# Experts' loads take places that come free piece by piece in the first stage; the inversion does both directions in one thread

## The chip, the cores and the metric

The kernel runs on one core of a Trainium2 chip. Its time is device time in microseconds, the median of 3 runs: 1031.37 us before the change (1030.21 to 1035.38).

## The reference, cut to what matters

All is float32, with 256 tokens of width 1024. A first block is a bidirectional gated delta rule (GDN) with an output projection and a LayerNorm, then 32 experts in 4 groups with top-1 group and top-2 experts, a LayerNorm and an embedding gate. A second block of two layers follows (an mLSTM layer and a sparse attention layer); the change does not touch what they compute.

```python
def _gated_delta_rule(q, k, v, beta, g):      # per chunk; once forward, once on the reversed sequence
    lhs = eye + jnp.einsum("nbhik,nbhjk->nbhij", kb, k) * decay * (1.0 - eye)
    u = solve(lhs, v * beta[..., None])        # unit lower triangular
    ...
x = _layernorm(ALPHA * x + gdn, ...)
for grp in range(4):                           # the experts
    h = silu(einsum("td,edf->tef", xt, w_gate[grp])) * einsum("td,edf->tef", xt, w_up[grp])
    out = out + einsum("tef,efd->td", h * comb[:, grp, :, None], w_down[grp])
x = _layernorm(ALPHA * x + out, ...)
x = x + sigmoid(x @ pe_w_gate) * (p @ pe_w_proj)
```

## The kernel before, in words

**Who sets the order.** The program is written as threads (Python generators) that a planner, `Sched` (L141), interleaves when the kernel is built. A thread asks for an engine (`yield "pe"`), waits for an event (`Wait`) or asks for buffers (`Alloc`); the planner keeps a modelled clock of each engine, of the DMA and of when each buffer comes free, picks the earliest thread (among nearly equal ones that of the smallest priority number), and writes its instructions out in that order. So a change of a modelled cost or of a buffer class can change the order of other work. On the chip each engine runs its instructions in the order written and waits by semaphores.

**Weights.** All weights come through one list of units of 1024 floats per partition (512 KB), loaded strictly in the list's order by one thread, `_load` (L488), on SP's queue. A unit asks for a place from the classes in its `places`. Dense weights are split by `_split` (L505) into a high and a low part in two places of class `hl`, and the raw place is free again; a unit marked late or full is used as it was loaded where the split doesn't come in time. Experts' weights (`m_gu`, 128 units, and `m_dn`, 64) are used as they are loaded. SP also issues the few other loads, among them x and two LayerNorm rows in `finish` (L1430).

**Places before.** 4 `raw` and 6 `hl` last for the whole program. 15 `moe_raw` and 4 `moe_hl` are opened by `moe_slots` (L470) in `hand_over` (L1367), when the GDN's buffers `la`, `e`, `t2`, `raw2` and `tap` are all done with. 8 more `moe_raw` (named `moe_raw_m` in the trace) and 2 `x_raw` are opened when the experts' stage begins. These are 39. The experts' units of the first two of eight steps may take `moe_raw` alone; the others take all classes, and wait for the last output-projection weights to be split. The residual r and the gathered tokens XG have buffers of their own.

**The first stage (GDN).** `main` (L1380) runs projections in the order of `GDN_ORDER` (L1475): q and k of head pairs 0 to 3, then v and z, then heads 4 to 7, z4 to z7, and the output projection o0 to o7. The heads are treated in two batches of four (`bt` 0 and 1). For each batch `base` (L1167) inverts 32x32 diagonal blocks column by column on VectorE (`columns`, L1210), `lev` (L1228) builds the 64x64 and 128x128 inverses from them by matmuls, and `solve` (L1305) applies them for each head pair; a solve frees the two `la` buffers of its pair, and the second batch's pairs take these. TensorE fills the rest with projections.

**The levels of the inversion.** `lev` is spawned four times, for 2 batches and 2 directions d. A step is a run of small matmuls into PSUM (class `bank`) and then evictions by ScalarE and VectorE, which the next step needs. Step 1: 32 matmuls of 32x32, half of them on one row group of the array, then half on another, all into the bank `px`. Step 2: per block two matmuls that read the same rows and write different columns, into banks `pt` and `pS`. Steps 3 and 4: 16 matmuls of 64x64 each, on one half of the rows. In the trace step 1 is `bank<-t,la`, step 2 `bank<-Tm,t` and `bank<-t,Tm`, step 3 `bank<-Tm,la`, step 4 `bank<-Sm,Tm`. A float32 matmul leaves two records.

**The experts' stage.** `Moe.main` (L2265): `ranks` and `group` make selection matrices, `gather` (L2092) collects up to 32 tokens per expert into XG, `up` (L2177) of step i multiplies them with 16 units of `m_gu` for four experts side by side on four column groups, `down` (L2198) with 8 units of `m_dn`, `scatter` adds to r. In the last `up`, `second_turn` (L2286) has a branch for crowded experts; at its end SP waits for all its loads, and only then the eight loads of `p_gate` for the embedding gate follow, into `raw` places.

Of the kernel before, what the change touches and what calls it, by code (L numbers as in the profile page):

```python
# [1 line left out]

# [43 lines left out]
MOE_RAW = 15  # L46
MORE_RAW = 8
# [93 lines left out]
class Sched:  # L141
# [60 lines left out]
    def mm(self, out, lhsT, rhs, first, last):  # L202
        self.nc.tensor.matmul(out, lhsT, rhs, start=first, stop=last, skip_group_check=True)  # L203
        n, m = size(rhs), size(lhsT)
        one = lhsT.dtype == F32R
        if n == 512 and m == 32:

            self.array(n, n)
            return
        self.array(max(n, 2 * m) if one else 4 * max(n, m) if n > 64 else 2.4 * n if m < 128 else max(4 * n, 2 * m),  # L210
                   (n if one else 4 * n) * rhs.shape[0] / 128.0, 0.0125 if one else 0.0025)
# [48 lines left out]

    def drop(self, *classes):
        for c in classes:
            del self.slots[c], self.pools[c]
# [33 lines left out]
    def _grant(self):  # L297

        again = True
        while again:  # L300
            again = False
            for t in sorted(self.threads, key=lambda t: (t.prio, t.seq)):
# [7 lines left out]
                elif isinstance(w, Alloc):  # L310
                    free = [s for c in (w.cls if isinstance(w.cls, tuple) else (w.cls,))
                            for s in self.slots.get(c, ())]
                    if len(free) >= w.n:
                        got = []
                        for s in sorted(free, key=lambda s: s.time)[:w.n]:
                            self.slots[s.cls].remove(s)
                            if isinstance(s.tag, int):
                                tile = self.pools[s.cls][:, s.tag]
# [59 lines left out]
class Unit:  # L378
# [4 lines left out]
    def __init__(self, name, src, more="", n=1024, whole=False, late=False, full=False,  # L383
                 places=None):
        self.name, self.src, self.more, self.n, self.whole, self.late = name, src, more, n, whole, late
        self.full, self.low, self.places = full, False, places or ("raw", more + "raw")
        self.sent, self.loaded = Event(), Event()
# [7 lines left out]
class Env:  # L395


    def __init__(self, tc, aps, ctx):
# [6 lines left out]
        self.res = ctx.enter_context(tc.tile_pool(name="res", bufs=1))  # L405
        S.slot_class("raw", self.wp, 4)
# [4 lines left out]
    def gate_slots(self):  # L411
# [4 lines left out]
        for x in s["gate_hl"]:  # L416
# [53 lines left out]
    def moe_slots(self):  # L470
# [3 lines left out]
        for cls, n in (("moe_raw", MOE_RAW), ("moe_hl", 4)):  # L474
# [6 lines left out]
    def start_weights(self, units, hold={}):  # L481

        self.units, self.at, self.hold = units, 0, hold
        for i, u in enumerate(units):
            u.index = i
        self.S.spawn(self._load(), 0)

    def _load(self):  # L488
# [15 lines left out]

    def _split(self, u):  # L505
        S = self.S
        hl = yield Alloc(("hl", u.more + "hl"), [1024], F32R, 2)
        yield Wait(u.loaded)
# [274 lines left out]
    def transposed(self, x, tb, h, l):  # L783

        yield Wait(*[self.S.spawn(self.turn(x, tb, h, l, c, Event()), 1) for c in (0, 4)])

    def turn(self, x, tb, h, l, c, done):
# [4 lines left out]
        for i in range(4):  # L792
            S.tr(p[:, i, :], x[:, tb, 128 * (c + i):128 * (c + i) + 128], self.ident)
# [84 lines left out]
class Gdn:  # L878


    def __init__(self, K, ctx):
# [5 lines left out]

        self.early = ExitStack()
        E = self.early.enter_context(K.stage("gdn_early", "right"))
        self.early_classes = ("la", "e", "t2", "raw2", "tap")  # L890
        for cls, n in zip(self.early_classes, (8, 4, 4, 4, 2)):
            K.S.slot_class(cls, E, n)
        K.S.slot_views("zx", K.res.tile([128, 4, 512], F32, name="x1", tag="x1"))
        self.LA, self.lev_ev, self.O = {}, {}, {}
# [10 lines left out]
        self.solved = [Event() for _ in range(8)]  # L905
# [169 lines left out]
    def qk_head(self, m, bank):  # L1075
# [18 lines left out]
        las = yield Alloc("la", [2, 3, 2, 128], n=2)  # L1094
# [6 lines left out]
        for d in range(2):  # L1101
            la = las[d]
# [64 lines left out]
    def base(self, bt):  # L1167
# [14 lines left out]
        tmp = yield Alloc("raw2", [512])  # L1182
# [45 lines left out]
    def lev(self, bt, d):  # L1228

        K, S = self.K, self.S  # L1230
        v, s, Sm, Tm = S.v, S.s, None, None
        yield Wait(self.base_ev[bt])
        Sm, Tm = self.Sm, self.Tm
        s32, t32 = self.AB if d == 0 else self.AB[::-1]
        u = slice(16 * d, 16 * d + 16)

        def lower(i):
            return self.LA[4 * bt + (i % 16) // 4, d][:, (i // 2) % 2, i % 2, 0]

        def span(pr):  # L1240
            return 64 * pr + 32 * d, 64 * pr + 32 * (1 - d)
# [8 lines left out]
        for pr, e in ((0, "act"), (1, "dve")):  # L1250
            f, t = span(pr)
            o = Tm[t:t + 32, u, 32 * d:32 * d + 32]
            yield e
            if pr:
                v.tensor_copy(o, px[t:t + 32])
            else:
                s.activation(o, px[t:t + 32], AF.Copy)
        S.free(px)
        yield Wait(self.diag_ev[bt])
        pt, pS = yield Alloc("bank", [16, 32], n=2)  # L1260
        for pr in range(2):
            f, t = span(pr)
            yield "pe"
            for i in range(16 * d, 16 * d + 16):
                x = Tm[t:t + 32, i, 32 * d:32 * d + 32]
                st = s32[t:t + 32, i, :]
                S.mm(pt[t:t + 32, i % 16, :], st, x, True, True)
                S.mm(pS[f:f + 32, i % 16, :], x, st, True, True)
        for pr in range(2):
            f, t = span(pr)  # L1270
            yield "act"
            s.activation(Tm[t:t + 32, u, 32 * d:32 * d + 32], pt[t:t + 32], AF.Copy, scale=-1.0)
            yield "dve"
            v.tensor_scalar(Sm[f:f + 32, u, t:t + 32], pS[f:f + 32], -1.0, None, op0=OP.mult)
        S.free(pt, pS)
        f, t = 64 * d, 64 * (1 - d)
        px = yield Alloc("bank", [8, 64], n=2)
        for half in range(2):
            yield "pe"
            for i in range(16 * d + 8 * half, 16 * d + 8 * half + 8):  # L1280
                S.mm(px[half][t:t + 64, i % 8, :], lower(i)[f:f + 64, t:t + 64], Tm[f:f + 64, i, :], True, True)
# [1764 lines left out]
```

## Time and profile before

| | |
|---|---|
| median of 3 runs | 1031.37 us |
| the profiled execution | 1031.94 us |
| its span | 1030.2 us |
| mean granted clock of TensorE | 0.972 |
| TensorE busy | 972.1 us (94%) |
| VectorE busy | 619.2 us (60%) |
| ScalarE busy | 484.9 us (47%) |
| bytes moved by DMA | 205.39 MB, mean 199 GB/s |

The span is what the profiler saw from the first to the last instruction; the execution's own time is 1.7 us longer. Times in the trace are microseconds from the span's start. Busy matmuls overlap, so TensorE's share is not its share of peak. A granted clock of 1.00 is 2.4 GHz, of 0.50 it is 1.2 GHz.

### The profile page before, as it was taken

To read this page: it belongs to the slowest core of one execution; us is meant where nothing else is said; L and a number is where in the kernel's file an instruction comes from. 1 tells how busy PE (TensorE), PEld (TensorE's weight loads), DVE (VectorE), ACT (ScalarE), POOL (GpSimd) and SP (SyncE) were. 2 spreads that over 40 slices of the span, in tenths; PEclk is the share of its full clock that TensorE was granted. 3 is DMA by queue.
4 is the path that set the end of the run, shared out by engine and by line. 5 is a ranking of instruction groups with operands and counts; after the bars stand their busy time and mean duration, and the time that the engine had idled before them with its cause. 6 is when DMAs were issued, how large, how long until landed. Compare 5 with 4: busy or idle time off the path is not lost. (4 is left out here: it accounts for less than half of the span.)

```text
span 1030.2 us, 17204 instructions
## 1 busy us (share of the span) xinstructions
PE 972.1 (94%) x6837; PEld 752.1 (73%) x6837; DVE 619.2 (60%) x1148; ACT 484.9 (47%) x897; POOL 114.2 (11%) x124
## 2 busy tenths in 40 slices
PE   8999989999899989999998788999999999998998
PEld 6778889888679765423221158999999988986886
DVE  7978865699944650221111086688677765687673
ACT  3888484794224422111110156576665444545561
POOL 2133130023000110000000050000000000004230
PEclk9999879999899989999999989999999999999999
DMA  6423411233332999999999953644554455732321
GB/s 222 144 82 104 143 43 42 63 123 102 123 104 77 408 416 381 416 414 416 415 415 415 403 191 127 202 150 162 165 163 157 158 176 164 257 114 71 123 83 41
DMA packets 56681, 205.39 MB, mean 199 GB/s; under 512 B 6417, under 2 KB 6801, under 8 KB 56209
## 3 DMA queue, kind: packets, MB, share of 16 engines
q1 hardware_dynamic: 56304, 204.02, 54.7%
q8 instruction: 56, 0.92, 0.4%
q10 hardware_dynamic: 288, 0.19, 0.1%
q14 instruction: 33, 0.26, 0.1%
HBM read 203.14 MB, written 1.05 MB: 198 GB/s over the span
## 5 line engine op out<-in xcount | busy, mean ns | idle before, releaser
L203 PE MATMUL dbank<-xh,hl 128*128 128x256 f32 x1072 | 216.4, 294 | 0.0
L203 PEld LDWEIGHTS dbank<-xh,hl 128*128 128x128 f32 x1072 | 173.7, 193 | 6.8 <-issue 4.9
L126 DVE TENSOR_TENSOR hl<-raw,hl 128x1024 fp32r<-128x1024 f32 x106 | 130.2, 1234 | 41.2 <-ACT hl L126 35.5
L203 PE MATMUL dbank<-xl,hl 128*128 128x256 f32 x536 | 152.7, 285 | 0.0
L126 ACT ACTIVATE hl<-raw 128x1024 fp32r<-128x1024 f32 x99 | 104.3, 1057 | 82.0 <-PE dbank L203 60.0
L203 PE MATMUL dbank<-hl,xh 128*128 128x256 f32 (+1 forms) x504 | 116.9, 317 | 0.9 <-ACT xh L126 0.9
L203 PEld LDWEIGHTS dbank<-xl,hl 128*128 128x128 f32 x536 | 103.8, 194 | 3.2 <-issue 3.1
L203 PEld LDWEIGHTS dbank<-hl,xh 128*128 128x128 f32 x504 | 86.6, 198 | 7.5 <-issue 1.9
L126 POOL TENSOR_TENSOR hl<-raw,hl 128x1024 fp32r<-128x1024 f32 x17 | 41.0, 2417 | 364.9 <-DMA raw<-in_p_gate 227.0
L203 PE MATMUL dbank<-hl,xl 128*128 128x256 f32 (+1 forms) x252 | 78.5, 312 | 1.4 <-DVE xl L126 1.3
L174 ACT ACT_TABLE_LOAD x53 | 68.0, 1283 | 0.9
L126 DVE SCALAR_TENSOR_TENSOR h<-h,cg,dbank 128x256 f32<-128x256 f32 x8 | 3.8, 479 | 83.4 <-ACT h L126 83.4
L203 PE MATMUL dbank<-xT,raw 128*128 128x256 f32 x240 | 53.0, 379 | 0.2 <-DMA raw<-in_g_qk 0.2
L203 PE MATMUL dbank<-moe_raw,XG 128*32 128x512 f32 x208 | 50.3, 599 | 2.8 <-DMA moe_raw<-in_m_gu 2.6
L203 PEld LDWEIGHTS dbank<-hl,xl 128*128 128x128 f32 x252 | 49.8, 198 | 4.0 <-DVE xl L126 2.1
L203 PEld LDWEIGHTS dbank<-xT,raw 128*128 128x128 f32 x240 | 45.2, 190 | 6.9 <-issue 1.0
L126 DVE TENSOR_TENSOR ys<-dbank,ys 128x512 fp32r<-128x512 f32 x16 | 11.0, 691 | 55.1 <-ACT ys L126 55.0
L126 ACT ACTIVATE h<-dbank 128x256 f32<-128x256 f32 x16 | 5.9, 383 | 78.0 <-PE dbank L203 78.0
L126 DVE TENSOR_TENSOR r<-r,bank 128x512 f32<-128x512 f32 x28 | 18.8, 686 | 38.2 <-PE bank L203 38.2
L126 ACT ACTIVATE ys<-dbank 128x512 fp32r<-128x512 f32 x16 | 9.4, 597 | 53.1 <-PE dbank L203 42.8
L126 ACT ACTIVATE XG<-bank 128x512 f32<-128x512 f32 x20 | 11.9, 597 | 43.5 <-PE bank L203 43.5
L203 PE MATMUL dbank<-hl,yh 128*128 128x512 f32 x96 | 31.1, 396 | 0.0
(447 smaller groups left out, 2068.9 us busy)
## 6 DMA issues: line engine op xcount, KB each, us to landing
moe_raw<-in_m_gu SPq DMA_DIRECT2D x52, 512.0 KB, 10.1
moe_raw<-in_m_dn SPq DMA_DIRECT2D x23, 512.0 KB, 10.1
hl<-in_m_gu SPq DMA_DIRECT2D x21, 512.0 KB, 9.9
moe_raw_m<-in_m_gu SPq DMA_DIRECT2D x20, 512.0 KB, 10.0
moe_raw_m<-in_m_dn SPq DMA_DIRECT2D x18, 512.0 KB, 10.2
raw<-in_g_qk SPq DMA_DIRECT2D x16, 512.0 KB, 4.6
raw<-in_g_z SPq DMA_DIRECT2D x16, 512.0 KB, 3.8
raw<-in_g_v SPq DMA_DIRECT2D x16, 512.0 KB, 3.8
```

Source lines behind the costliest of these rows:

```text
L126: r = f(*a, **k)
L174: self.nc.scalar.preload_act_table_set(t)
L203: self.nc.tensor.matmul(out, lhsT, rhs, start=first, stop=last, skip_group_check=True)
```

## The change

- The GDN's buffers x, `e`, `raw2` and `tap` become parts of one tile `first` of 7680 floats; when all decays, all v and the last z projection are done (`first_places`), it is opened again as 7 places. `la` is 4 buffers of a pair instead of 8, and when all are handed out each freed one is opened as 3 places (`more_places`).
- `MOE_RAW` 15 becomes 0, `MOE_HL` is 2 instead of 4, `MORE_RAW` 8 becomes 10, and `x_raw` has 4 places instead of 2: 45 places with the 19 of `first`, the 4 `raw` and the 6 `hl`. All experts' units may use all (`RAWS`); until the last output-projection weights are split, `_open` keeps them to `moe_raw` and `first`.
- r, XG, the embedding's products (pp) and x2 take places of these classes (2 each) instead of buffers of their own.
- `p_gate` may load into `raw` and `first`; splits of the mLSTM layer's weights wait until the gate's splits have their places.
- `lev` is one thread for both directions. In each step the matmuls of both directions and both block pairs alternate; the evictions are threads of their own, and the next step waits for all of them. `base` takes its scratch tile from `t4`.
- The planner's cost of a small matmul is 2 max(n, 48) cycles instead of 2.4 n.

```diff
-MOE_RAW = 15
-MORE_RAW = 8
+MOE_RAW = 0
+MOE_HL = 2
+RAWS = ("moe_raw", "moe_hl", "raw", "hl", "first", "x_raw")
+MORE_RAW = 10
...
-        ... else 2.4 * n if m < 128 else ...
+        ... else 2 * max(n, 48) if m < 128 else ...
...
     def _load(self):
         for u in self.units:
-            if u.name == "m_gu" and len(u.places) > 1:
-
-                yield Wait(*[v.ready for v in self.units[0:u.index] if v.name == "g_out" and not v.late])
-            u.raw = yield Alloc(u.places, [1024])
+            a = self.asks = Alloc(u.places, [1024])
+            if u.places is RAWS and not self.opened:
+                a.cls = ("moe_raw", "first")
+            u.raw = yield a
...
+        K.first = K.first_ctx.enter_context(K.stage("gdn_first", "right"))
+        t = K.first.tile([128, 7680], F32, name="first0", tag="first")
+        self.x = t[:, 0:2048].rearrange("p (k n) -> p k n", k=8)
+        for cls, at, size, n in (("e", 2048, 768, 4), ("raw2", 5120, 512, 4), ("tap", 7168, 256, 2)):
+            K.S.slot_parts(cls, t, at, size, n)
...
+    def first_places(self):
+        S = self.S
+        yield Wait(*self.la_ev.values(), *self.v_ev, self.z_done)
+        S.drop("e", "raw2", "tap")
+        S.more_views("first", self.K.first.tile([128, 7, 1024], F32, name="first1", tag="first"))
+
+    def more_places(self):
+        S = self.S
+        yield Wait(*self.la_ev.values())
+        for i in range(4):
+            t = yield Alloc("la", [3, 1024])
+            S.more_views("first", t)
...
-    def lev(self, bt, d):
+    def lev(self, bt):
...
+        four = [(pr, d, *span(pr, d)) for d in range(2) for pr in range(2)]
         px = yield Alloc("bank", [16, 32])
-        yield "pe"
-        for pr in range(2):
-            f, t = span(pr)
-            for i in range(16 * d, 16 * d + 16):
-                S.mm(px[t:t + 32, i % 16, :], lower(i)[f:f + 32, t:t + 32], t32[f:f + 32, i, :],
-                     True, True)
...
+        for h in range(2):
+            yield "pe"
+            for i in range(8 * h, 8 * h + 8):
+                for pr, d, f, t in four:
+                    S.mm(px[t, i, :], lower(d, i)[f, t], AB[d][1][f, 16 * d + i, :], True, True)
+        yield Wait(*[S.spawn(evict(("act", "dve")[pr], Tm[t, u[d], 32 * d:32 * d + 32], px[t]), "lev")
+                     for pr, d, f, t in four])
...
+        p = yield Alloc("bank", [16, 32], n=2)
+        for h in range(2):
             yield "pe"
+            for i in range(8 * h, 8 * h + 8):
+                for pr, d, f, t in four:
+                    x = Tm[t, 16 * d + i, 32 * d:32 * d + 32]
+                    st = AB[d][0][t, 16 * d + i, :]
+                    S.mm(p[d][t, i, :], st, x, True, True)
+                    S.mm(p[d][f, i, :], x, st, True, True)
...
+        two = [(d, slice(64 * d, 64 * d + 64), slice(64 - 64 * d, 128 - 64 * d)) for d in range(2)]
+        p = yield Alloc("bank", [8, 64], n=2)
         for half in range(2):
             yield "pe"
+            for i in range(8 * half, 8 * half + 8):
+                for d, f, t in two:
+                    S.mm(p[half][t, i % 8, :], lower(d, i)[f, t], Tm[f, 16 * d + i, :], True, True)
...
-        X = yield Alloc("XG", [8, 256])
+        self.XGt[g] = yield Alloc(RAWS, [1024], F32, 2)
...
+        self.r = yield Alloc(RAWS, [1024], F32, 2)
...
-        return Unit(name, src, "moe_", full=True, places=("moe_raw",) if i < 2 else ("moe_raw", "moe_hl", "raw", "hl", "x_raw"))
+        return Unit(name, src, "moe_", full=True, places=RAWS)
...
-    ... "gate_") for i in range(4) for h in range(2)]
+    ... "gate_", places=("raw", "first")) for i in range(4) for h in range(2)]
```

## Rows read from the trace of the kernel before

**Rows 1.** The page's slices: GB/s in 40 equal slices of the span.
```profile
GB/s 222 144 82 104 143 43 42 63 123 102 123 104 77 408 416 381 416 414 416 415 415 415 403 191 127 202 150 162 165 163 157 158 176 164 257 114 71 123 83 41
```

**Rows 2.** Windows: length, busy time (instructions) per engine, PEclk, DMA share, GB/s.
```profile
320.00:330.00 10.00, 10.00 (x69) 8.60 (x69) 4.08 (x8) 4.82 (x8) 0.00 (x0) 1.00 0.01 2
390.00:400.00 10.00, 10.00 (x76) 5.31 (x69) 0.00 (x0) 1.62 (x3) 0.00 (x0) 1.00 0.91 328
```

**Rows 3.** SP's timeline around T0: start, length, the loads that it issues.
```profile
329.27 0.33 SPq L228 DMA_DIRECT2D xt<-in_x  x1
...
334.75 13.76 SPq L228 DMA_DIRECT2D moe_raw<-in_m_gu  x12
...
380.89 1.61 SPq L228 DMA_DIRECT2D x_raw<-in_m_dn  x2
389.83 0.33 SPq L228 DMA_DIRECT2D moe_raw<-in_m_dn  x1
```

**Rows 4.** Timeline of all engines from 365 to 392 us.
```profile
367.40 0.69 DVE L126 SCALAR_TENSOR_TENSOR t<-xt,dbank 128x512 f32<-128x512 f32 x1 [3.21 <-PE dbank L203]
...
378.43 9.11 PE L203 MATMUL bank<-sel,x 128*128 128x256 f32 x32 [0.35 <-DVE sel L126]
...
387.90 4.50 PE L203 MATMUL dbank<-moe_raw,XG 128*32 128x512 f32 x40
```

**Rows 5.** SP's timeline behind the experts' loads.
```profile
594.75 1.85 SPq L228 DMA_DIRECT2D raw<-in_p_gate  x4
```

**Rows 6.** Windows over the first stage: PE, PEld, DVE, ACT, POOL busy, PEclk.
```profile
158.00:205.00 47.00, 47.00 (x351) 41.39 (x350) 29.21 (x53) 29.84 (x55) 0.06 (x1) 1.00 0.15 46
205.00:240.00 35.00, 34.61 (x225) 29.16 (x224) 33.05 (x65) 32.44 (x63) 11.35 (x6) 1.00 0.29 91
240.00:271.00 31.00, 31.00 (x132) 24.50 (x131) 28.43 (x70) 9.66 (x15) 6.30 (x7) 1.00 0.47 151
271.00:275.50 4.50, 0.62 (x2) 0.00 (x0) 4.36 (x7) 0.00 (x0) 0.00 (x0) 1.00 0.60 203
275.50:287.00 11.50, 11.44 (x141) 10.11 (x142) 8.09 (x20) 2.77 (x4) 0.00 (x0) 0.55 0.19 63
287.00:307.00 20.00, 19.48 (x408) 15.52 (x407) 9.78 (x12) 6.19 (x10) 0.00 (x0) 1.00 0.27 84
307.00:367.40 60.40, 60.26 (x368) 50.84 (x366) 32.15 (x49) 24.48 (x35) 4.52 (x4) 1.00 0.68 263
```

**Rows 7.** TensorE's groups, 121 to 158.6 us: count | busy us, mean ns | idle before.
```profile
L203 PE MATMUL bank<-Tm,la 64*64 64x64 f32 x64 | 5.7, 266 | 0.0
L203 PE MATMUL bank<-t,la 32*32 32x32 f32 x128 | 5.3, 217 | 2.3 <-DVE t L126 2.3
L203 PE MATMUL bank<-Tm,t 32*32 32x32 f32 x128 | 5.1, 207 | 0.0
...
L203 PE MATMUL bank<-Sm,Tm 64*64 64x64 f32 x64 | 4.1, 220 | 0.0
```

**Rows 8.** TensorE's groups, 275 to 307 us.
```profile
L203 PE MATMUL bank<-t,la 32*32 32x32 f32 x128 | 5.8, 226 | 3.9 <-DVE t L126 3.9
...
L203 PE MATMUL bank<-Tm,la 64*64 64x64 f32 x64 | 4.3, 220 | 0.5 <-issue 0.5
L203 PE MATMUL bank<-Sm,Tm 64*64 64x64 f32 x64 | 4.2, 220 | 0.0
...
L203 PE MATMUL bank<-Tm,t 32*32 32x32 f32 x128 | 4.0, 192 | 0.0
```

**Rows 9.** Windows of 0.1 us, TensorE's matmuls of step 1 alone.
```profile
276.30:276.40 0.10, 0.10 (x9) 1.00 0.30 123
...
276.50:276.60 0.10, 0.10 (x12) 0.81 0.20 82
```

**Rows 10.** ScalarE's groups, 275 to 307 us.
```profile
L126 ACT ACTIVATE Tm<-bank 32x512 f32<-32x512 f32 x6 | 3.5, 588 | 13.1 <-PE bank L203 13.0
```

**Rows 11.** VectorE's groups, 275 to 307 us.
```profile
L126 DVE TENSOR_SCALAR Sm<-bank 32x512 f32<-32x512 f32 x4 | 2.7, 687 | 1.3 <-PE bank L203 1.2
```

More of the change, by code (lines that the diff above doesn't have):

```diff
@@ L503, in _load, with _open @@
                 self.S.spawn(self._split(u), self.S.tune["split"])
+    def _open(self):
+        yield Wait(*[v.ready for v in self.units if v.name == "g_out" and not v.late])
+        self.opened = True
+        if self.asks.cls == ("moe_raw", "first"):
+            self.asks.cls = RAWS
     def _split(self, u):
         S = self.S
+        if u.more == "even_":
+            yield Wait(*[v.parted for v in self.units[0:u.index] if v.more == "gate_"])
         hl = yield Alloc(("hl", u.more + "hl"), [1024], F32R, 2)
+        S.set(u.parted)
         yield Wait(u.loaded)
@@ new lines, in lev, with lower, evict, span @@
+        AB = self.AB, self.AB[::-1]
+        u = [slice(16 * d, 16 * d + 16) for d in range(2)]
+        def lower(d, i):
+            return self.LA[4 * bt + i // 4, d][:, (i // 2) % 2, i % 2, 0]
+        def evict(e, o, p, scale=None):
+            yield e
+            if e == "act":
+                s.activation(o, p, AF.Copy, scale=scale or 1.0)
+            elif scale:
+                v.tensor_scalar(o, p, scale, None, op0=OP.mult)
+            else:
+                v.tensor_copy(o, p)
+        def span(pr, d):
+            return slice(64 * pr + 32 * d, 64 * pr + 32 * d + 32), slice(64 * pr + 32 - 32 * d, 64 * pr + 64 - 32 * d)
@@ L1278, in lev @@
+        yield Wait(*[S.spawn(evict(*x, -1.0), "lev") for pr, d, f, t in four
+                     for x in (("act", Tm[t, u[d], 32 * d:32 * d + 32], p[d][t]), ("dve", Sm[f, u[d], t], p[d][f]))])
+        S.free(*p)
+        two = [(d, slice(64 * d, 64 * d + 64), slice(64 - 64 * d, 128 - 64 * d)) for d in range(2)]
+        p = yield Alloc("bank", [8, 64], n=2)
         for half in range(2):
             yield "pe"
-            for i in range(16 * d + 8 * half, 16 * d + 8 * half + 8):
-                S.mm(px[half][t:t + 64, i % 8, :], lower(i)[f:f + 64, t:t + 64], Tm[f:f + 64, i, :], True, True)
@@ L1291, in lev @@
+        yield Wait(*[S.spawn(evict(("act", "dve")[half], Tm[t, 16 * d + 8 * half:16 * d + 8 * half + 8, :], p[half][t]),
+                             "lev") for half in range(2) for d, f, t in two])
+        S.free(*p)
+        p = yield Alloc("bank", [8, 64], n=2)
         for half in range(2):
             yield "pe"
-            for i in range(16 * d + 8 * half, 16 * d + 8 * half + 8):
-                S.mm(pS[half][f:f + 64, i % 8, :], Tm[t:t + 64, i, :], Sm[t:t + 64, i, t:t + 64], True, True)
@@ L1305, in solve @@
+        yield Wait(*[S.spawn(evict(("act", "dve")[half], Sm[f, 16 * d + 8 * half:16 * d + 8 * half + 8, t], p[half][f],
+                                   -1.0), "lev") for half in range(2) for d, f, t in two])
+        S.free(*p)
+        for d in range(2):
+            S.set(self.lev_ev[bt][d])
     def solve(self, bt, ml):
@@ L2056, in ranks @@
         S.set(self.rg_ev)
-        S.spawn(self.group(0), "ranks")
-        S.spawn(self.rest(), "rest")
         yield "pe"
@@ L2268, in main @@
         self.done = []
+        S.spawn(self.group(0), -1)
+        S.spawn(self.rest(), -1)
         S.spawn(self.ranks(), "ranks")
@@ L2378, in norm @@
             self.K.bn(st, n, r[n])
-        yield from self.K.layernorm(r, [u.raw for u in us], self.x2[:, tb], st, self.bn_ev[tb], 2 * tb + 1)
+        yield from self.K.layernorm(r, [u.raw for u in us], self.x2[tb], st, self.bn_ev[tb], 2 * tb + 1)
         self.S.free(*r)
@@ L2403, in moe_units @@
         out += (gu(i) if i < 8 else []) + (dn(i - 1) if i > 0 else [])
-    return out + [Unit("p_gate", lambda i=i, h=h: a["p_gate"][i, :, 4 * h:4 * h + 4], "gate_") for i in range(4) for h in range(2)]
+    return out + [Unit("p_gate", lambda i=i, h=h: a["p_gate"][i, :, 4 * h:4 * h + 4], "gate_", places=("raw", "first")) for i in range(4) for h in range(2)]
 class Embed:
```

188 lines of the change are left out of this document (88 added, 100 removed).

## The prediction

> **What bounds the kernel now.** I read the page's slices first: for about ten slices in the middle the DMA engines move some 415 GB/s and nothing more can be had from them [rows 1]. The windows of 10 us around the beginning of that stretch show where it opens (2 GB/s in 320 to 330 us) and one dent, 328 GB/s between 390 and 400 us [rows 2]. SP's own timeline explains the dent: the experts' loads are issued in nine groups, x12 first and x2 last, 39 loads in all, then SP issues nothing between 382.5 and 389.83 us [rows 3]. That is the moment at which all 39 places are full, and it is also the moment at which the first expert matmul (387.90 us) has read its first four tiles [rows 4]. So before 388 us the stream is limited by places, after 390 us by the 415 GB/s. A load is 0.524 MB, 1.26 us at that rate; 192 loads of expert weights and 4.5 others (the embedding's p and its projection, two LayerNorm rows) make 196.5, so 157.5 remain, 199 us, plus 1.9 us of the dent: 389.8 + 201 = 591, and the first load behind the stream (p_gate), which waits for the last landing, is issued at 594.75 us [rows 5]. From there to the end of the span are 1030.2 - 594.8 = 435.4 us, which the diff touches only at their beginning.
>
> The end therefore follows from two numbers: T0, the time of the first expert matmul, and the number of loads that are already in places at T0. What sets T0 is read backwards in the timeline: gather for group 0 at 378.43, LayerNorm of the second half at 367.40, behind the last output matmul [rows 4]; from 275.5 to 367.4 us TensorE is busy all the time, and before that it waits 3.9 us for VectorE, which has been at the triangular inversion's columns since 240 us [rows 6]. So T0 hangs on TensorE's work after 275.5 us, on that VectorE chain, and on what comes before it.
>
> **The change, part by part.**
>
> *Places that come free earlier.* 7 places come free when the last z matmul has read x (by 271.6 us), 3 more with each of the last four solves, which follow the second inversion (307 us), where 15 now come together, the first of them used for experts at 334.75 us [rows 3]. This alone moves no end: the stream already fills every place by T0 and would only be full sooner. It is needed so that an earlier T0 also finds full places: 41 loads take 52 us and x and the LayerNorm rows 5 us more, so for a T0 of 376 us the stream has to begin by about 319 us. I cost it at nothing, between 0 and a loss of 1.26 us for each load that is missing at T0. The loads of x and the rows, at 329.27 us now [rows 3], will queue behind experts' loads, up to eight deep, some 10 us; they are wanted at about 356 us, so this is covered.
>
> *The number of places.* 45 in all, of which r takes 2 and the gathered tokens of group 0 take 2: 41 at T0 instead of 39. Two loads fewer to come after T0: -2.5 us. The tokens of the next group take their two later, when places are plentiful.
>
> *The inversion.* Before, each direction is a thread of its own, and its matmuls go in runs that use the same rows of the array. Its TensorE time in the first batch of heads: 5.3 + 5.1 + 5.7 + 4.1 = 20.2 us [rows 7]; in the second: 5.8 + 4.0 + 4.3 + 4.2 = 18.3 us [rows 8]. (The two 32x32 groups of the middle step run at the same time, so they count once; each matmul is two records.) After, neighbours in program order use different rows and different columns. What the trace shows of such neighbours: in the middle step now, pairs with the same rows and different columns: 128 matmuls in 4.0 us, 31 ns each; the first step, same rows and same columns, 64 matmuls in 5.8 us, 91 ns each. For different rows there is one place, where the first step goes over from one row group to the next: there 12 records are under way in 0.1 us instead of 9 [rows 9], into one PSUM bank. So I take the pair's 31 ns for the first step (64 x 31 = 2.0 us), no gain for the middle step (4.0), and two at once for the 64x64 steps (half of 8.5 = 4.2): 10.2 us; with 0.8 for the part that falls at the lower clock 11.0 us. Bounds: all row groups at once and four in the first and middle step, 1.0 + 2.0 + 4.2 = 7.2 us; none at once, today's 18.3 to 20.2 us. Saved: 7.3 us in the second batch, 9.2 in the first.
>
> How much of it reaches T0? The second batch's whole: between 275.5 and 367.4 us TensorE never rests, and the output projection's matmuls that now stand between the steps fill the waits. Of the first batch's I take half, 4.6 us: TensorE is full until 271 us, but from 205 to 240 us VectorE and ScalarE are at 94% and 93% as well, and from 240 to 275.5 us VectorE's chain goes on in its own time [rows 6]. Bounds: 0 and 9.2.
>
> The evictions stay the same in number. They now come four, eight, four and four at a time, half on each engine, and the next step waits for all: at 0.59 us on ScalarE and 0.69 on VectorE [rows 10, 11] 1.4 + 2.8 + 1.4 + 1.4 = 7.0 us per inversion. I cost this at nothing because the output matmuls (TensorE is busy 30.9 of the 31.5 us from 275.5 to 307 [rows 6], so 12.6 us of it are not the inversion) and the projections of the first batch fill it; without that cover it is 7.0 us twice.
>
> By the Trainium skill ("TensorEngine Tiling (Array Packing)", "Gotcha 1: PSUM Pressure") "different row tiles cannot access same PSUM bank simultaneously"; all four row groups of the new first step write one bank. By that rule the inversion would gain nothing, and the sum would be -2.5 us. The 12 records against 9 speak against it, over a tenth of a microsecond.
>
> *The rest.* The four output-projection loads wait less for raw places, but their split tiles have 8 places instead of 10: 0, between -1 and +2 us. The p_gate loads may go to 23 places instead of 4; after their first one is issued TensorE's next run starts with the second LayerNorm, so 0, between -2 and +1. A new plan reorders other work by a little: 2 us either way.
>
> *Sum.* T0: -7.3 - 4.6 = -11.9, so 376.0 us; two loads: -2.5. Against the profiled execution, 1031.94 us (1030.2 us of span and 1.7 around it): 1017.5. The median of the runs is 0.6 us lower, 1031.37, so I forecast 1017.
>
> **Rivals.**
> 1. *Only the second inversion counts* (20%): the first one's time is lost between VectorE and ScalarE at 205 to 275 us. For it: 94% and 93%; against: the 100% of TensorE from 158 to 205 us at unhurried other engines. -7.3 - 2.5: 1022.
> 2. *The row groups don't run beside each other* (15%): matmuls of different row groups that write one bank go one after the other, as each direction's first step does now at 91 ns. For it: nowhere does the trace hold them side by side for longer than the 0.1 us of [rows 9]; against: that tenth of a microsecond. Then T0 stays and the two places remain: 1031.4 - 2.5 = 1029. This is the case of the Trainium skill's rule above.
> 3. *Slower: the two directions in lockstep* (11%). Place: the four waits for evictions in each inversion, 7.0 us; now one direction's matmuls run during the other's evictions. If nothing is there to fill them TensorE idles 14 us over both, and after its idle time at 271 us the clock was granted at 0.55 in the next 11.5 us [rows 6], so idling costs more than itself. It decides from the point at which idle time exceeds what is saved: with rival 2's condition at once, 1031.4 + 14 - 2.5 = 1043; otherwise beyond 16.5 us. Against it: TensorE idles 0.5 us between 287 and 307 us.
> 4. *The early places are the gain* (4%): the stream starts with 19 places some 40 us earlier and keeps that lead of 19 x 1.26 = 24 us to its end: 1007. Against it: the pause at 382.5 us; a lead ends where places are full.
>
> **How the numbers follow.** The forecast holds 50%, with a range of its own from 1010 to 1023 (the saved times between half and all, the small terms at their ends). For 8 in 10 I leave out most of rival 3 and the extreme of rival 4: 1007 to 1031, which includes rivals 1 and 2. About 0.5% (5 us) is what a measurement here tells from no change. Faster by more: 50 + 20 + 4, less 1 for the forecast's edge = 0.73. Within: 0.16 (rival 2 and that edge). Slower: 0.11.
>
> **What would show it.** In the profile after: experts' loads issued well before 320 us, a pause of SP before T0 longer than today's 7 us, or of the same length with T0 earlier; the first expert matmul near 376 us; the inversion's groups at about 11 us for each batch instead of 20.2 and 18.3 us; p_gate issued near 580 us and some 435 us from there to the end. Wrong would be: the 32x32 and 64x64 groups no shorter (rival 2), TensorE idle inside 275 to 300 us (rival 3), T0 moved by 7 us or less with short groups (rival 1), or an end that moves by much more than T0 does (rival 4).

## The result

The changed kernel takes 1019.17 us (median of 4 runs, 1018.12 to 1019.82), the kernel before 1033.05 in the same comparison: a ratio of 0.9863, 95% interval 0.9837 to 0.9890. The forecast was 1017 us, with a range of 1007 to 1031. The profiled execution has a span of 1018.0 us, 12.2 less than before.

First the page of the kernel after, GB/s in 40 slices of the span, against [rows 1]:

```profile
GB/s 224 146 83 105 163 33 56 63 104 125 277 106 327 212 369 397 409 409 409 408 410 407 334 194 117 179 164 156 160 146 166 166 185 164 255 111 104 84 95 51
```

The slices before the plateau (the long row of nearly equal rates) hold loads that came all together before the change (277 106 327 212 369), and the plateau ends earlier: 334 where 403 stood. But it is lower, 409 where it was 415.

Windows of the kernel after (columns as in [rows 2]: length, PE, PEld, DVE, ACT, POOL busy, granted clock, DMA share, GB/s):

```profile
320.00:330.00 10.00, 10.00 (x45) 8.10 (x44) 7.30 (x11) 7.41 (x10) 1.29 (x1) 1.00 1.02 413
330.00:340.00 10.00, 10.00 (x45) 8.20 (x45) 4.88 (x4) 3.18 (x3) 0.00 (x0) 1.00 0.23 91
...
370.00:380.00 10.00, 10.00 (x78) 5.39 (x80) 0.00 (x0) 4.17 (x6) 0.00 (x0) 1.00 0.82 319
...
410.00:500.00 90.00, 84.96 (x453) 30.99 (x446) 18.30 (x32) 12.39 (x28) 0.00 (x0) 1.00 1.03 409
```

The stream is at full rate in 320 to 330 us, where it stood before, and then nearly stops: 91 GB/s. SP's timeline of the kernel after says why (start, length, loads; against [rows 3, 5]):

```profile
301.25 9.22 SPq L232 DMA_DIRECT2D la<-in_m_gu  x6
312.12 0.33 SPq L232 DMA_DIRECT2D xt<-in_x  x1
...
326.11 13.69 SPq L232 DMA_DIRECT2D first<-in_m_gu  x3
339.85 1.85 SPq L232 DMA_DIRECT2D raw<-in_m_gu  x4
...
366.44 0.33 SPq L232 DMA_DIRECT2D xh_raw<-in_m_gu  x1
376.14 0.80 SPq L232 DMA_DIRECT2D first<-in_m_gu  x2
...
581.34 1.29 SPq L232 DMA_DIRECT2D la<-in_p_gate  x3
```

Loads go out at 301 us, before x's at 312; from 326 to 340 SP waits for places (three loads in 13.7 us); the last of 41 goes out at 366.44, and nothing more until 376.14. That pause of 9.4 us has the same reason as the one of 7.3 us before: every place is full, and the first comes free when the first expert matmuls have read it. TensorE's timeline of the kernel after (against [rows 4]):

```profile
363.64 10.20 PE L207 MATMUL bank<-sel,x 128*128 128x256 f32 x32 [0.55 <-DVE sel L130]
...
374.20 0.62 PE L207 MATMUL dbank<-first,moe_raw_m 128*32 128x512 f32 x2
```

So T0 is 374.20 us (before 387.90; forecast 376.0), `p_gate` is issued at 581.34 (before 594.75), and from there to the end it is 1018.0 - 581.3 = 436.7 us (before 435.4). The 12.2 us of the span are 13.7 at T0, less 0.3 between T0 and `p_gate`, less 1.3 behind it.

The inversion's groups on TensorE, kernel after (count | busy us, mean ns | idle before), first batch, against [rows 7]:

```profile
L207 PE MATMUL bank<-t,Tm 32*32 32x32 f32 x128 | 3.2, 218 | 2.2 <-issue 2.2
L207 PE MATMUL bank<-Tm,t 32*32 32x32 f32 x128 | 3.2, 218 | 2.6 <-DVE Tm L130 1.5 <-ACT Tm L130 1.0
...
L207 PE MATMUL bank<-Sm,Tm 64*64 64x64 f32 x64 | 2.2, 221 | 0.2 <-ACT Tm L130 0.2
L207 PE MATMUL bank<-Tm,la 64*64 64x64 f32 x64 | 2.1, 220 | 0.0
...
L207 PE MATMUL bank<-t,la 32*32 32x32 f32 x128 | 1.3, 193 | 2.4 <-DVE t L130 2.4
```

and second batch, against [rows 8]:

```profile
L207 PE MATMUL bank<-Tm,t 32*32 32x32 f32 x128 | 2.8, 219 | 0.0
L207 PE MATMUL bank<-t,Tm 32*32 32x32 f32 x128 | 2.8, 219 | 1.9 <-issue 1.9
L207 PE MATMUL bank<-Tm,la 64*64 64x64 f32 x64 | 2.1, 220 | 0.0
L207 PE MATMUL bank<-Sm,Tm 64*64 64x64 f32 x64 | 2.1, 220 | 0.0
L207 PE MATMUL bank<-t,la 32*32 32x32 f32 x128 | 1.9, 237 | 3.6 <-DVE t L130 3.6
```

The two groups of step 2 run at the same time, so the first inversion takes TensorE 1.3 + 3.2 + 2.1 + 2.2 = 8.8 us (before 20.2), the second 1.9 + 2.8 + 2.1 + 2.1 = 8.9 (before 18.3). Step 1 is 128 records in 1.3 us, 10 ns each, with four row groups writing one bank; before it was 5.3 us. Not all of that is the order of the matmuls, since before the clock was at its lower level for part of step 1. Windows of 1 us with step 1's matmuls alone, all three at a granted clock of 1.00, of the kernel before (one row group), of e12 below (two by turns) and of the kernel after (four by turns):

```profile
121.60:122.60 1.00, 1.00 (x40) 1.00 0.27 107
121.60:122.60 1.00, 1.00 (x72) 1.00 0.38 152
121.60:122.60 1.00, 1.00 (x126) 1.00 0.19 74
```

At one and the same clock there are three times as many records, and their number rises with the number of row groups that take turns.

Windows of the first inversion, kernel before (those of the second are in [rows 6]):

```profile
121.00:135.00 14.00, 12.15 (x303) 11.85 (x303) 7.80 (x14) 10.23 (x23) 4.81 (x7) 0.76 0.30 97
135.00:148.00 13.00, 11.66 (x165) 11.13 (x166) 10.16 (x22) 9.95 (x19) 5.64 (x6) 0.61 0.14 43
```

and of both inversions, kernel after:

```profile
121.00:135.00 14.00, 7.59 (x408) 6.87 (x408) 11.58 (x24) 13.26 (x28) 7.56 (x10) 0.85 0.28 97
135.00:148.00 13.00, 11.77 (x163) 9.97 (x164) 8.08 (x16) 12.21 (x22) 3.45 (x3) 0.77 0.13 43
240.00:267.80 27.80, 24.20 (x99) 17.97 (x97) 25.91 (x60) 8.09 (x10) 2.34 (x1) 0.99 0.60 207
267.80:275.50 7.70, 7.65 (x229) 6.27 (x232) 7.57 (x19) 2.01 (x3) 0.00 (x0) 0.58 0.86 343
275.50:287.00 11.50, 9.60 (x267) 7.87 (x254) 6.93 (x9) 4.67 (x8) 1.30 (x2) 0.70 0.35 109
287.00:307.00 20.00, 19.98 (x195) 17.84 (x194) 10.21 (x18) 7.54 (x12) 0.00 (x0) 1.00 0.37 131
```

TensorE waits 3.6 us ahead of the second inversion, as before (3.9). New is idle time within the inversions: 6.4 of the first 14 us of the first one (before 1.9), 1.9 of 11.5 us in the second (before 0.1). In the second the granted clock is 0.58 and 0.70 (before 0.55 over 11.5 us): behind the idle time it was at the lower of its two levels (1.2 GHz) for more than half of these stretches. In the first it is 0.85 and 0.77, higher than before, for all the idle time.

### The profile page after: what moved, and what is told of

The parts are those of the page before. It is cut to its first block, busy times and chain, and to the rows that moved or that the text cites. A ratio compares the mean times of both kernels' runs of the same rounds, so it can differ in the third digit from the quotient of the medians.

```text
span 1018.0 us, 17221 instructions
## 1 busy us (share of the span) xinstructions
PE 956.3 (94%) x6841; PEld 734.4 (72%) x6841; DVE 612.6 (60%) x1132; ACT 485.1 (48%) x904; POOL 136.4 (13%) x140
## 5 line engine op out<-in xcount | busy, mean ns | idle before, releaser
L130 DVE TENSOR_TENSOR hl<-raw,hl 128x1024 fp32r<-128x1024 f32 x100 | 122.7, 1233 | 37.2 <-ACT hl L130 34.9
L130 ACT ACTIVATE hl<-raw 128x1024 fp32r<-128x1024 f32 x90 | 94.8, 1057 | 71.0 <-PE dbank L207 44.3
L207 PE MATMUL dbank<-hl,xh 128*128 128x256 f32 (+1 forms) x512 | 121.2, 321 | 1.0 <-ACT xh L130 1.0
L207 PEld LDWEIGHTS dbank<-hl,xh 128*128 128x128 f32 x512 | 89.2, 200 | 8.2 <-issue 1.9
L207 PE MATMUL dbank<-first,raw 128*128 128x256 f32 (+1 forms) x260 | 61.7, 402 | 0.2 <-DMA first<-in_m_gu 0.2
L207 PEld LDWEIGHTS dbank<-first,raw 128*128 128x128 f32 (+1 forms) x260 | 47.0, 185 | 8.9 <-DMA first<-in_m_gu 1.8
L130 DVE TENSOR_TENSOR t<-t,t 128x31 f32<-128x31 f32 (+15 forms) x124 | 47.7, 385 | 4.3
L130 DVE TENSOR_TENSOR moe_raw_m<-moe_raw_m,bank 128x512 f32<-128x512 f32 x28 | 18.9, 685 | 47.8 <-PE bank L207 47.8
L130 POOL TENSOR_TENSOR hl<-la,hl 128x1024 fp32r<-128x1024 f32 x3 | 7.1, 2371 | 228.0 <-DMA la<-in_p_gate 228.0
L207 PE MATMUL bank<-sel,x 128*128 128x256 f32 x128 | 32.1, 410 | 0.6 <-DVE sel L130 0.6
## 6 DMA issues: line engine op xcount, KB each, us to landing
la<-in_m_gu SPq DMA_DIRECT2D x40, 512.0 KB, 10.2
first<-in_m_gu SPq DMA_DIRECT2D x23, 512.0 KB, 10.2
hl<-in_m_gu SPq DMA_DIRECT2D x20, 512.0 KB, 10.2
moe_raw_m<-in_m_gu SPq DMA_DIRECT2D x20, 512.0 KB, 10.2
```

The source lines that it names most:

```text
L130: r = f(*a, **k)
```

## The experiments

In each, "before" was run beside it. First to last is the time from the start of the inversion's first matmul to the end of its last; T0, the issue of `p_gate` and the span are those of one execution, the profiled one. Seven of these kernels have the same inversion (after, e1, e3, e4, e7, e8, e11), and their T0 lies between 371.1 and 375.2 us: a difference of less than 4 us in T0 shows little by itself.

| kernel | ratio to before [95%] | inversion 1, first to last | inversion 2, first to last | T0 | `p_gate` | span |
|---|---|---|---|---|---|---|
| before | 1 | 121.3 to 158.5 | 275.6 to 306.2 | 387.9 | 594.7 | 1030.2 |
| after | 0.9863 [0.9837, 0.9890] | 121.4 to 147.7 | 267.8 to 290.4 | 374.2 | 581.3 | 1018.0 |
| e1 levels alone | 0.9879 [0.9855, 0.9903] | 122.5 to 148.7 | 268.9 to 289.8 | 373.7 | 582.2 | 1019.1 |
| e2 places alone | 1.0005 [0.9991, 1.0020] | 122.7 to 161.5 | 278.3 to 308.4 | 387.8 | 594.7 | 1030.5 |
| e3 places late | 0.9870 [0.9847, 0.9893] | 122.3 to 148.5 | 269.0 to 290.9 | 373.9 | 581.3 | 1019.4 |
| e4 eight fewer | 0.9977 [0.9963, 0.9992] | 121.9 to 148.2 | 268.4 to 289.2 | 372.6 | 590.3 | 1028.3 |
| e5 same rows | 0.9937 [0.9922, 0.9952] | 121.3 to 150.7 | 270.9 to 297.3 | 381.1 | 587.5 | 1027.0 |
| e6 second batch | 0.9903 [0.9883, 0.9923] | 122.1 to 152.3 | 272.5 to 293.4 | 376.6 | 582.8 | 1021.8 |
| e7 constants | 0.9826 [0.9808, 0.9843] | 121.8 to 148.1 | 268.7 to 291.2 | 375.2 | 579.1 | 1015.8 |
| e8 all at 256 | 0.9819 [0.9801, 0.9838] | 121.2 to 147.5 | 267.7 to 288.5 | 371.1 | 573.5 | 1010.2 |
| e9 two halves | 0.9926 [0.9899, 0.9952] | 121.5 to 146.7 | 267.8 to 292.3 | 378.5 | 585.0 | 1021.6 |
| e10 halves, 256 | 0.9870 [0.9846, 0.9893] | 122.4 to 147.8 | 268.9 to 293.7 | 377.3 | 580.1 | 1016.4 |
| e11 old cost | 0.9866 [0.9841, 0.9892] | 121.4 to 149.4 | 268.9 to 292.1 | 374.3 | 580.9 | 1017.2 |
| e12 two threads | 1.0046 [1.0030, 1.0063] | 121.5 to 154.8 | 269.8 to 302.6 | 388.7 | 596.6 | 1034.8 |

**e1, the inversion alone** (the kernel before with the new `lev` and its cost):

```diff
-    def lev(self, bt, d):   # two threads
+    def lev(self, bt):      # as in the change; places as before
```

> The kernel before with the new inversion alone (one thread for both directions, neighbours on different rows, the planner's new cost for them); places as before, 39, all at once behind the last solve. Theory (the end follows from T0 and from the loads in places at T0): T0 moves as in the changed kernel, some 13.7 us to about 374; the places come free some 13 us earlier too, since the last solve follows the inversion; 39 loads and x need 54 us from 321, so they are just in, and the time is 11 us under the kernel before (two loads, 2.5 us, less than the whole change), 8 if the stream is not quite full at T0. Rival 'early places are the gain': no more than 3 us under before.

T0 is 373.7 and the median 1019.78 us against 1031.67 before: 11.9 us, nearly the whole gain.

**e2, the places alone** (the changed kernel with the old `lev` and cost):

> The changed kernel with the old inversion (a thread for each direction, runs on the same rows, the old cost); its 45 places come free piece by piece. Theory: T0 stays within 1 us of 387.9, SP's pause before it grows, and two loads more are in: 2.5 us under the kernel before, between 0 and 4. Rival 'early places are the gain': 10 us or more under it. If the two parts need each other, the sum of this gain and of the inversion's alone is well under the 13.9 us of the whole.

T0 is where it was and the time is 0.05% over before, interval 0.09% under to 0.20% over. The 2.5 us of the two places are not there: the changed kernel's places bring the lower plateau with them (409 GB/s here too, 415 in e1). 155.5 loads of 0.524 MB cost 0.0185 us more each at 409 than at 415, 2.9 us. From T0 to `p_gate` it takes 206.9 us, as before.

**e3, the same places, handed over late** (behind the last solve, as before):

```diff
-        yield Wait(*self.la_ev.values(), *self.v_ev, self.z_done)   # first_places
+        yield Wait(*self.o_ev)
-        yield Wait(*self.la_ev.values())                            # more_places
+        yield Wait(*self.o_ev)
```

> The changed kernel, its 19 pieces handed over only behind the last solve, at once, as before; 45 places and the new inversion stay. Theory: the stream begins near 321 us, 41 loads and x need 57 us, so T0 near 374 finds two to four loads missing: 0 to 4 us over the changed kernel, T0 the same within 2 us. Rival 'early places are the gain': 10 us over it or more.

T0 373.9, time as the changed kernel's. The first experts' load goes out at 318.8 instead of 286.9 us, and still 41 are issued by 369.9, 5.9 us before places come free. Coming free early is worth nothing at this T0.

**e4, eight places kept back until T0 is past:**

```diff
-            S.more_views("first", t)
+            S.more_views("first", t[:, 0:1])
+            kept.append(t[:, 1:3])
...
+        yield Wait([u for u in self.K.units if u.places is RAWS][46].sent)
+        for t in kept:
+            S.more_views("first", t)
```

> The changed kernel with eight of the late pieces (two of three in each of the four) kept back until the 47th expert load is sent, so that 33 and not 41 loads can be in places at T0. Theory: T0 as in the changed kernel within 1 us, the end 8 x 1.26 to 1.28 = 10 us later, 24 us over... that is 10 us over the changed kernel and some 3 to 4 us under the kernel before. If places at T0 do not count (the stream's end set by TensorE), within 2 us of the changed kernel.

From T0 to `p_gate` it takes 217.7 us instead of 207.1: 10.6 us for eight loads, 1.32 each. The number of full places at T0 does set the end.

**e5, one thread, old order of matmuls** (all of one row group, then the next):

```diff
-                for pr, d, f, t in four:
-                    S.mm(px[t, i, :], ...)                 # i outside, rows inside
+            for i, (pr, d, f, t) in turns(range(16), four, h):
+                S.mm(px[t, i, :], ...)                     # rows outside, i inside
```

> The changed kernel, with the matmuls of each step of the inversion in the old order: all of one row group, then all of the next. One thread, its waits and its planner's cost stay. Theory (neighbours on different rows run beside each other): the groups are as long as before the change (5.3 to 5.8, 4.0 to 5.1 and twice 4.1 to 4.3 us), T0 between 383 and 393 us, the time 9 to 19 us over the changed kernel; more than 14 over it means that one thread in lockstep by itself is worse than two. If the one thread or the new planner's cost made the gain: within 3 us of the changed kernel.

T0 is 381.1: 6.9 us later than in the changed kernel, but 6.7 us earlier than in e2, whose matmuls have the same order in two threads. So the order of the matmuls is only half of the gain. The clock did not make the other half: from 118 us to T0 it was at its lower level for 41.0 us in e2 and for 37.6 us in e5, which is 1.7 us of TensorE's work. (e2 also has the planner's old cost; e11 tests that, but in the changed kernel.) What one thread does is seen in the 64x64 steps of the first inversion. The view of the tile Tm of e2 (count, duration of a matmul min/median/max, first and last start):

```profile
L207 PE MATMUL bank<-Tm,la x64: 218/289/366, 143.1 to 156.9; 64*64 64x64 f32 x64
L207 PE MATMUL bank<-Sm,Tm x64: 218/218/267, 150.9 to 161.3; 64*64 64x64 f32 x64
```

of e5:

```profile
L207 PE MATMUL bank<-Tm,la x64: 218/218/267, 142.2 to 145.4; 64*64 64x64 f32 x64
L207 PE MATMUL bank<-Sm,Tm x64: 218/218/267, 147.3 to 150.5; 64*64 64x64 f32 x64
```

and of the kernel after:

```profile
L207 PE MATMUL bank<-Tm,la x64: 217/218/267, 141.4 to 143.3; 64*64 64x64 f32 x64
L207 PE MATMUL bank<-Sm,Tm x64: 217/218/267, 145.5 to 147.5; 64*64 64x64 f32 x64
```

In two threads one direction's steps 3 and 4 come behind the other's: from 143.1 to 161.3 us with four trips to the evictions (a trip is a wait until a step's results have been moved out of PSUM). In one thread both directions make each trip together, and the same matmuls run from 142.2 to 150.5 us. Each row group's run now also overlaps the next one's first matmuls (64 records in 3.4 us; in e2 32 take 2.1): over both inversions the 64x64 groups take 13.8 us of TensorE's time, in e2 18.1. How the 6.7 us divide between the trips and this overlap is not shown.

**e6, the new order in the second batch only:**

> The changed kernel with the old order of matmuls in the first batch's inversion only; the second's keeps the new one. Theory by the trace (the second inversion begins 7.7 us earlier in the changed kernel): T0 and the time 7 to 9 us later than the changed kernel. By the half that the prediction took: 4.6 us. Rival 1 (only the second counts): within 1.5 us of the changed kernel.

None of the three: T0 is 2.4 us later and the median 3.2. The first inversion is 4.0 us longer and the second begins 4.7 us later, but it then takes 20.9 instead of 22.5 us. If these figures are taken as they are, the first batch has 2.4 of the 6.9 us that the order gives T0 (e5), and the second 4.5. But 376.6 is only 1.4 us later than the latest T0 of the seven kernels with the whole new inversion, and the ratio's interval overlaps that of the changed kernel: that the first batch counts is likely, how much is not shown.

**e7, the constants' side back at a multiple of 256 bytes.** The change allocates `lg`, 288 bytes, among the constants, ahead of `raw`, `hl`, xh and xl. It moves these 14 places by 288 bytes. That they began at a multiple of 256 bytes before is taken from the kernels' own allocation; the traces hold no addresses. The windows of the kernel before show two rates: six loads into `hl` land from 423.9 to 430.0 us, eight into `moe_raw_m` (by the allocation not at a multiple of 256) from 432.5 to 441.5:

```profile
424.00:430.00 6.00, 6.00 (x48) 1.69 (x44) 2.58 (x6) 0.39 (x1) 0.00 (x0) 1.00 1.03 423
432.00:442.00 10.00, 10.00 (x67) 6.44 (x66) 1.38 (x2) 3.58 (x6) 0.00 (x0) 1.00 1.03 413
410.00:540.00 130.00, 121.20 (x639) 42.96 (x638) 26.96 (x46) 19.01 (x46) 0.00 (x0) 0.99 1.03 415
```

```diff
-        self.lg = K.const.tile([128, 2, 36], F32, name="lg")
+        self.lg = K.const.tile([128, 2, 64], F32, name="lg")[:, :, 0:36]
```

> The changed kernel with 224 bytes more in the tile lg of the constants: the change had put lg (288 bytes) ahead of the places raw, hl, xh and xl, which before lay at a multiple of 256 bytes and then at 32 beyond one; now they lie at a multiple of 256 again, 14 of 45 places. Theory (a load into a place at a multiple of 256 bytes lands every 1.23 us, into another every 1.28): these places' loads land every 1.23 us, the stream moves 413 to 416 GB/s instead of 409, the time is 2.5 to 3.5 us under the changed kernel. Rival (the pieces of the first stage are the slower places): 409 GB/s, no change.

The window of e7:

```profile
410.00:540.00 130.00, 121.84 (x610) 41.38 (x608) 26.96 (x45) 17.55 (x37) 0.00 (x0) 1.00 1.03 415
```

415 GB/s again; from T0 to `p_gate` 203.9 us instead of 207.1, where the seven other kernels with the changed kernel's places have 206.2 to 207.9. The median is 3.4 us under the changed kernel's, the span 2.2; the ratios' intervals just overlap, so the saving rests on the rate and on that stretch. **e8** pads the other places as well (224 bytes ahead of the pieces, 160 ahead of the MoE stage's tiles):

> The changed kernel with pads of 224 bytes behind the constants, 224 ahead of the pieces and 160 ahead of the MoE stage's own tiles, so that 43 of the 45 places lie at a multiple of 256 bytes. Theory: nearly all loads land every 1.23 us, some 426 GB/s, 155 loads x 0.05 = 8 us under the changed kernel if TensorE keeps up; if TensorE bounds there before that, 3 to 6. If only the places of the constants' side differ, 3. Rival (the address has nothing to do with it): no change.

```profile
410.00:540.00 130.00, 122.04 (x601) 40.78 (x594) 26.15 (x44) 17.57 (x37) 0.00 (x0) 1.00 1.03 419
```

419, not 426: three loads of four now land 1.23 to 1.25 us apart, but every fourth still 1.28, whatever its place. What makes the fourth is open. From T0 to `p_gate` 202.5 us, 4.7 less than after. e8 is the fastest kernel of the study: 1013.99 us, 5 under the changed kernel. Shown is that the shift counts: with these places moved by 0 (e1) or by 512 bytes (e7) the plateau is 415 GB/s, by 288 it is 409, and e8's pads add to it. That 256 bytes is the multiple that matters, and not a larger or smaller one, was not tested.

By the Trainium skill ("DMA: Bandwidth & Descriptors", "How a descriptor splits into AXI transactions") a transfer is cut at multiples of 256 bytes, and one that doesn't start at such a multiple begins with a transaction from the multiple below it. The page tells this of what is read; these places are written to. Worked out from that, an estimate, a row of 4096 bytes that starts 32 bytes beyond a multiple has 17 transactions instead of 16, 6%. The direction agrees with e7 and e8, the size doesn't: 419 against 409 GB/s is 2.4%.

**e9 and e10, the inversion in two halves of eight heads**, so that one half's matmuls fill the other's evictions (e10 with the pads of e8):

```diff
-            self.lev(bt)
+            self.lev(bt, h)   # for h in range(2): heads 8 h to 8 h + 7 of both directions
```

> The changed kernel with the inversion cut in two threads of eight heads each (both directions and all row groups in each), so that one half's matmuls can run during the other half's evictions; 12 more evictions per inversion, of half the length. Theory A (the waits for evictions, some 18 of the first inversion's 26.3 us, are what is left): the first inversion takes 20 to 23 us, the second 17 to 19, T0 and the time 4 to 8 us under the changed kernel. Theory B (VectorE and ScalarE bound the inversion, busy 11.6 and 13.3 of the 14 us from 121): 25 to 28 and 21 to 23 us, the time within 2 us of the changed kernel.

> Two halves as in e9, and the pads of e8. If the two are independent, its distance to the changed kernel is the sum of theirs: e8's 5 us and what e9 gives.

Theory A fell, and theory B fits the first inversion alone (25.2 us; the second takes 24.6, and the time is 4.6 us over the changed kernel's). The first inversion ends 1.0 us earlier than in the changed kernel and the second 1.9 us later; T0 is 4.3 us later. The window of e9 at the second one:

```profile
268.00:290.00 22.00, 15.63 (x494) 12.81 (x484) 15.84 (x33) 5.93 (x15) 0.00 (x0) 0.62 0.45 164
```

and the same of the kernel after:

```profile
268.00:290.00 22.00, 20.09 (x536) 16.45 (x534) 15.53 (x28) 7.35 (x11) 1.30 (x2) 0.70 0.54 197
```

TensorE is idle for 6.4 of these 22 us in e9, for 1.9 in the kernel after, and e9's clock is the lower one. e10 is 5.3 us under e9 by the medians, as the pads alone.

**e11, the planner's old cost:**

> The changed kernel with the planner's old cost for the 32x32 and 64x64 matmuls (2.4 times the columns instead of 2 times max(columns, 48)). It only orders the work. Theory: within 1.5 us of the changed kernel. If the planner's cost is what moved the rest of T0 that the order of the matmuls did not (6.7 of 13.7 us in e5): 4 to 8 us over it.

1018.48 us, T0 374.3. With one thread the cost orders nothing that counts.

**e12, the new order in two threads:**

```diff
-        for pr in range(2):
-            for i in range(16 * d, 16 * d + 16):
+        for i in range(16 * d, 16 * d + 16):
+            for pr in range(2):
```

> The changed kernel with the old inversion in two threads, one for each direction, but with the matmuls of its two 32x32 steps in the new order within a direction (two row groups by turns instead of one after the other); the 64x64 steps as before the change. Beside e2 (two threads, old order) and e5 (one thread, old order) it separates the two edits. Theory 'order and thread add': two row groups at once save up to half of 10.4 us in the first inversion and of 9.8 in the second, T0 4 to 7 us under e2's 387.8, the time 1026 to 1029. Theory 'the thread is what counts' (the round trips to the evictions, made once for both directions): T0 within 2 us of e2's, the time 1030 to 1033.

T0 is within 2 us of e2's, as the second theory has it, but for another reason, and the time is even over its range (1.0046; behind `p_gate` it is 438.2 us instead of e2's 435.8). At the start of the second inversion e12 is ahead, 269.8 instead of 278.3 us, in part by the clock: around the first inversion it was at its lower level for 10.2 us in e12 and for 23.9 us in e2. In the second inversion TensorE has idle time, and the clock stays low. Windows of e12:

```profile
267.00:274.00 7.00, 4.17 (x131) 3.92 (x132) 6.96 (x15) 1.18 (x2) 0.00 (x0) 0.75 1.03 416
274.00:290.00 16.00, 13.23 (x306) 10.72 (x306) 9.58 (x15) 2.83 (x5) 0.00 (x0) 0.50 0.35 122
290.00:306.00 16.00, 16.00 (x106) 14.15 (x106) 2.92 (x4) 2.66 (x4) 1.30 (x2) 0.50 0.04 10
```

0.50 over 32 us. The last two of these windows in e2:

```profile
274.00:290.00 16.00, 12.32 (x162) 9.52 (x162) 13.18 (x24) 4.24 (x5) 0.00 (x0) 0.79 0.78 307
290.00:306.00 16.00, 16.00 (x364) 12.59 (x356) 6.20 (x9) 4.13 (x7) 1.30 (x2) 0.89 0.13 44
```

The view of Tm in e12 shows the 64x64 matmuls at 311 ns:

```profile
L207 PE MATMUL bank<-Tm,la x64: 311/311/365, 281.3 to 295.9; 64*64 64x64 f32 x64
L207 PE MATMUL bank<-Sm,Tm x64: 311/311/366, 289.1 to 302.3; 64*64 64x64 f32 x64
```

In the kernel after their median is 218. 32 us at half the clock cost up to 16 us of TensorE's work, against 5.1 in e2: enough to take back the 8.5 us by which the second inversion began earlier. It is no accident of one execution: the mean granted clock is 0.958 to 0.965 in all six runs of e12 and 0.966 to 0.973 in the twelve of e2. What the order is worth in two threads at e2's clock was not measured.

## Why the prediction was right, point by point

- **What bounds the kernel: right.** Full places before T0, the rate after it. e2 to e4 bear it out: T0 and the places in use at T0 set `p_gate`. But that nothing more than 415 GB/s can be had is too strong: e8 has 419 over 130 us.
- **Early places alone: 0, right** (e3; rival 4 is out with it and with e2). The early start only puts a wait in the middle: SP stands 13.7 us for places from 326 us, and nobody waits for that.
- **Two more places: -2.5 us, right in size (e4), but not alone.** What the prediction lacked is a term of +2.9 us: 288 bytes of constants moved 14 places, and the plateau fell from 415 to 409 GB/s. The forecast held the rate fixed.
- **TensorE's time in the inversion: too cautious.** 11.0 us each were forecast, 8.8 and 8.9 came; step 2 gained as well (4.0 to 2.8 us, taken as no gain), and two row groups by turns do as much there (2.5 us in e12's first inversion). The two prices that the forecast set side by side were of two clocks: step 1's 91 ns a matmul fall in the stretch at 0.55 [rows 6], step 2's 31 ns in one at 1.00. At 1.00 step 1's records start 30 ns apart in the kernel before, 60 ns a matmul. By the Trainium skill's rule ("TensorEngine Tiling (Array Packing)", "Gotcha 1: PSUM Pressure") four row groups that write one bank could not use it at the same time; three times the records at one clock (x126 against x40) say that here they do. Rival 2 is out with it.
- **How much of it reaches T0: the step that failed, though its sum held.** The prediction gave T0 the second batch's saving whole (7.3) and half of the first's (4.6), 11.9 in all, and put all of it down to the order of the matmuls. T0 moved by 13.7 us, of which e5 gives 6.9 to the order, 5.0 less than forecast, and 6.7 to the single thread, which was costed at nothing. That the sum at T0 was off by 1.8 us only is luck. The split holds with the thread put in first; in two threads the order gave T0 nothing (e12). Of TensorE's 20.8 us saved 7 never reach T0; some of them are idle time (9.7 of the 47 us from 118 to 165, before 5.3).
- **Evictions at nothing, rival 3 as their price: wrong in sign.** The lockstep was thought to cost up to 7.0 us per inversion; it takes half of the trips to the evictions away. TensorE's idle time came as rival 3 said, 6.4 and 1.9 us, but the 9 to 11 us of matmuls saved in each inversion covered it. The clock did not fall with it in the first inversion (0.85 and 0.77, before 0.76 and 0.61); around the second, from 265 to 320 us, it is 0.88 where it was 0.91. e12 is what rival 3's clock looks like when the saving does not cover it.
- **Rival 1** (only the second counts) is unlikely, but not clearly out: in the changed kernel the first inversion ends 10.8 us earlier and the second starts 7.7 earlier, but e6 leaves the first batch's order only 2.4 us at T0, which is within the scatter of T0.
- **The rest: 0 forecast, +1.3 behind `p_gate`**, within its bounds.

So the sum was -11.9 - 2.5 = -14.4 and came out at -12.2 on the span (-13.9 by the medians): T0 gave 1.8 more than forecast, the rate took 2.9 back and the tail 1.3 (0.2 remain). Three errors met in the sum: the order gave 5.0 less than forecast, one thread 6.7 more, and the rate took 2.9.

## What to carry to other kernels

Where a stream of loads waits for places and a stage end sets when they come free, the count of places at that moment and the moment itself are the price; making places free earlier than they can be filled is not. Merging two threads that make the same round trips to other engines was worth as much here as the better order of the matmuls (6.7 and 6.9 us of T0), though how much of it is the trips is not shown: count the trips, not only the engine's time. Compare two prices only at one granted clock. After moving any buffer, look at the plateau of the transfer rate: a small tile ahead of large ones can cost as much as two places bring.

## What the runs showed of the hardware, not expected

- Matmuls of 32x32 on four row groups by turns, all into one PSUM bank (different partitions): in 1 us of step 1 at a granted clock of 1.00 there are 126 records, 72 with two row groups by turns (e12) and 40 with one (before). At 0.50 it is 86 (after, 268 to 269 us), 52 (e12, 271 to 272) and 27 (before, 276.6 to 277.6).
- Loads of 128 rows of 4096 bytes move at a rate that depends on where the places lie: 423 GB/s in a window in which loads into `hl` land, 413 in one with `moe_raw_m`; over 130 us 419 with e8's pads, 409 with the places of the changed kernel.
- With TensorE busy 17.4 of the 23 us from 267 to 290 us in pieces, the granted clock was 0.75 and then 0.50, and stayed at 0.50 through 16 us more in which it was busy all the time (e12).
